# Weight operands kept as two pairs of tiles, raw-block products first, and the gated embedding added onto the output in DRAM

## The chip, the cores and the metric

The kernel runs on one NeuronCore of a Trainium2 chip: TensorE (PE) for matmuls, VectorE (DVE), ScalarE (ACT), GpSimd (POOL), and SyncE (SP), which here only issues DMAs. The metric is the device time of one execution in microseconds (us), as the median of the runs.

## The reference

One layer of a hybrid encoder for 640 tokens (512 of a prompt, 128 of samples): an input projection, attention beside a state-space group, and then the part that matters here, four large projections in fp32.

```python
merged = jnp.concatenate([rms_norm(attn, g_attn_out), rms_norm(ssm, g_ssm_out)], axis=-1)
h = x + merged @ w_out
f = rms_norm(h, g_ffn)
h = h + (jax.nn.silu(f @ w_gate) * (f @ w_up)) @ w_down
gate = jax.nn.sigmoid(rms_norm(h, g_ple) @ w_ple_gate)
h = h + gate * (p_i @ w_ple_proj)
```

D_MODEL is 2048 and D_FF 5632, so the weights of these four stages are 16 to 46 MB each and are read once.

## The kernel before

Up to about 806 us the kernel does the input projections, the attention and the state-space group. From there on it is one long sequence of 2x2 block multiplications by the Strassen-Winograd scheme: seven products in place of eight. The stages are called after the tiles that their products write: **o** (w_out, 8 cells of 4 units), **g** and **u** (w_gate and w_up, 22 pairs of cells of 4 units each), **d** (w_down, 28 cells of 2 to 4 units, the last eight with a longer ending), **p** (w_ple_gate, 8 cells of 4 units). That makes 87 cells that end in the function `strassen`, and a last one, p7, with code of its own.

A *unit* is a 128x1024 block of weights: four 128x256 quarters, loaded by SP into `wst` (two buffers, L60). For each unit:

- POOL makes three of the four weight sums in `ws` (L109, L110, L111), DVE the fourth (L112). `ws` has one buffer.
- ACT rounds each part to fp32r (`wh`, L86), and DVE takes the remainder (`wl`, L87). This is done once for the three raw quarters (128x768, straight from `wst`) and once for the four sums (128x1024, from `ws`). Below, these are the raw split and the sum split. Both write into one pair of tiles `wh`, `wl` of seven blocks, with two buffers: the pair of unit i+2 can be written only when PE is through with unit i.
- PE does seven products of six matmuls each, 42 matmuls of 128x320 per unit (L1205 to L1207). Products 1, 2 and 4 need raw quarters, products 3, 6, 7 and 5 need sums. The order is 1, 2, 3, 6, 7, 5, 4.

So the weights pass round a ring: POOL's three sums, ACT's sum split, DVE's sum split, and only then POOL's sums of the next unit, since `ws` has one buffer. Each product accumulates in its own PSUM bank over the units of a cell; there are eight banks. When a cell ends, the banks are read and combined (L1232 to L1240): 1 and 3 by ACT, the others by DVE, with one addition on POOL at the end (L1240). Then comes the stage's own ending: a row scale on DVE (`by_rows`, L1257), for g a Silu on ACT (L1307), for u a multiplication by g's tile on DVE (L1317) and four row sums on POOL (L118 to L121); for d an addition to `h_dr` in DRAM by a DMA that POOL issues (L1346), or in the last eight cells an addition, a scaling, squares and the row sums; for p a sigmoid (L1367), a multiplication by the projected embedding on DVE (L1370), the addition of the residual on POOL (L1373), and the store of the output.

The instructions are written cell by cell, but the order on each engine is set by a scheduler that runs at build time. Within an engine the instructions run strictly in that order.

## Time and profile before

| | |
|---|---|
| median of 3 runs | 3037.12 us (3029.13 to 3037.15) |
| the profiled execution, its own time | 3029.73 us |
| its span, first to last instruction | 3027.9 us |
| PE busy | 2850.7 us (94%) |
| DVE / POOL / ACT busy | 2042.4 / 1540.3 / 1237.7 us |
| mean granted TensorE clock | 0.983 of full |

The page's share of busy time says that PE is nearly always at work, but matmuls overlap in it, and its ends are modelled. Where PE stands still is better read from the start times of its matmuls: in an undisturbed run they start at an even distance, and what a stretch takes beyond its number of matmuls times that distance is lost. The page's chain of work that ended last passes through POOL for 23%, DVE for 15% and PE for 12% of the span.

### The profile page before, as it was taken

How to read it: one execution, taken by the hardware profiler on the slowest of the kernel's cores; microseconds unless marked ns; L12 is line 12 of the kernel's file. 1: busy time of each engine (PE TensorE's matmuls, PEld its weight loads, DVE VectorE, ACT ScalarE, POOL GpSimd, SP SyncE). 2: the span in 40 equal slices, each digit the busy share in tenths (PEclk: the TensorE clock that was granted, in tenths of full speed). 3: DMA queues.
4: the chain of work that ended last, by engine and by line, in shares of the span. 5: the costliest groups of instructions: out<-in, count | busy, mean ns of one | idle time of the engine just before them, and what ended most of it. 6: DMA issues, size and time to landing. Idle time of an engine off the chain costs nothing.

```text
span 3027.9 us, 48370 instructions
## 1 busy us (share of the span) xinstructions
PE 2850.7 (94%) x19051; PEld 2719.3 (90%) x19051; DVE 2042.4 (67%) x2830; ACT 1237.7 (41%) x1627; POOL 1540.3 (51%) x1545
## 2 busy tenths in 40 slices
PE   7899999999789889999999999999989999988898
PEld 6789988888788889999999999999989999987887
DVE  8939254455777786666666666666775667788766
ACT  4333365456633443333333333333434344444432
POOL 5612300000666665656565656565564554666665
PEclk9999999999899999999999999999999999999999
DMA  5565744456444623232323232323555455646443
GB/s 165 155 172 168 227 173 154 173 200 209 169 150 159 244 85 117 98 118 98 117 99 115 99 115 99 114 99 114 213 127 164 110 171 164 168 155 243 135 146 129
DMA packets 137494, 449.24 MB, mean 148 GB/s; under 512 B 14097, under 2 KB 34673, under 8 KB 124465
## 3 DMA queue, kind: packets, MB, share of 16 engines
q1 hardware_dynamic: 120032, 396.47, 38.6%
q0 software_dynamic: 15936, 45.47, 6.0%
q10 hardware_dynamic: 1296, 4.20, 0.4%
q8 instruction: 149, 2.44, 0.3%
q14 instruction: 81, 0.66, 0.1%
HBM read 342.25 MB, written 101.18 MB: 146 GB/s over the span
## 4 chain that ended last, share of the span: by engine, by line
POOL 23%; DVE 15%; PE 12%; issue 8%; ACT 6%; DMA 1%; DVEq 0%; POOLq 0%; SPq 0%; ACTq 0%
POOL ws L110 7%; DVE wl L87 7%; POOL ws L109 6%; ACT wh L86 5%; POOL ws L111 5%; PE d L1207 4%; PE d L1205 4%; PE d L1206 4%; POOL t L121 1%; POOL t L118 1%; DVE t L1257 1%; DVE rg L1257 1%; POOL rp L1373 1%; DVE kt L1051 1%; POOL t L120 1%
## 5 line engine op out<-in xcount | busy, mean ns | idle before, releaser
L86 ACT ACTIVATE wh<-ws 128x1024 fp32r<-128x1024 f32 x328 | 347.2, 1058 | 976.4 <-POOL ws L111 957.9
L87 DVE TENSOR_TENSOR wl<-ws,wh 128x1024 fp32r<-128x1024 f32 x328 | 415.9, 1268 | 488.2 <-ACT wh L86 488.0
L109 POOL TENSOR_TENSOR ws<-wst 128x256 f32<-128x256 f32 x328 | 335.4, 1023 | 758.1 <-DVE wl L87 758.1
L87 DVE TENSOR_TENSOR wl<-wst,wh 128x768 fp32r<-128x768 f32 x328 | 413.7, 1262 | 94.3 <-ACT wh L86 94.2
L1205 PE MATMUL d<-kt,wh 128*128 128x320 f32 x1232 | 384.9, 315 | 27.2 <-ACT wh L86 15.2
L1207 PE MATMUL g<-kf,wl 128*128 128x320 f32 x1232 | 380.6, 313 | 15.8 <-DVE wl L87 15.6
L1205 PE MATMUL g<-kf,wh 128*128 128x320 f32 x1232 | 382.1, 311 | 3.5 <-ACT wh L86 3.5
L1205 PE MATMUL u<-kf,wh 128*128 128x320 f32 x1232 | 380.7, 309 | 3.4 <-ACT wh L86 3.3
L1206 PE MATMUL d<-kt,wh 128*128 128x320 f32 x1232 | 381.9, 312 | 0.0
L1206 PE MATMUL g<-kf,wh 128*128 128x320 f32 x1232 | 381.4, 310 | 0.0
L1206 PE MATMUL u<-kf,wh 128*128 128x320 f32 x1232 | 380.3, 309 | 0.0
L1207 PE MATMUL u<-kf,wl 128*128 128x320 f32 x1232 | 379.4, 311 | 0.3 <-DVE wl L87 0.3
L1207 PE MATMUL d<-kt,wl 128*128 128x320 f32 x1232 | 362.6, 314 | 13.1 <-DVE wl L87 13.0
L110 POOL TENSOR_TENSOR ws<-ws,wst 128x256 f32<-128x256 f32 x328 | 357.3, 1089 | 23.1
L86 ACT ACTIVATE wh<-wst 128x768 fp32r<-128x768 f32 x328 | 275.0, 839 | 224.0 <-PE d L1206 74.2
L111 POOL TENSOR_TENSOR ws<-wst,ws 128x256 f32<-128x256 f32 x328 | 289.8, 884 | 21.2
L1205 PEld LDWEIGHTS d<-kt,wh 128*128 128x128 f32 x1232 | 234.8, 191 | 34.1 <-ACT wh L86 20.2
L1207 PEld LDWEIGHTS g<-kf,wl 128*128 128x128 f32 x1232 | 231.5, 189 | 22.9 <-DVE wl L87 22.2
L1207 PEld LDWEIGHTS d<-kt,wl 128*128 128x128 f32 x1232 | 228.6, 191 | 19.0 <-DVE wl L87 18.4
L1205 PEld LDWEIGHTS g<-kf,wh 128*128 128x128 f32 x1232 | 232.5, 189 | 5.3 <-ACT wh L86 5.2
L1205 PEld LDWEIGHTS u<-kf,wh 128*128 128x128 f32 x1232 | 231.3, 188 | 4.2 <-ACT wh L86 4.2
L1206 PEld LDWEIGHTS d<-kt,wh 128*128 128x128 f32 x1232 | 234.9, 191 | 0.0
(501 smaller groups left out, 6489.9 us busy)
## 6 DMA issues: line engine op xcount, KB each, us to landing
wst<-in_w_gate SPq DMA_DIRECT2D x88, 512.0 KB
wst<-in_w_up SPq DMA_DIRECT2D x88, 512.0 KB
wst<-in_w_down SPq DMA_DIRECT2D x88, 512.0 KB
tc_dr<-t SPq DMA_DIRECT2D x22, 1120.0 KB
kt<-tc_dr SPq DMA_DIRECT2D x22, 1120.0 KB
wst<-in_w_qk SPq DMA_DIRECT2D x32, 512.0 KB
kc<-in_cache_k SPq DMA_DIRECT2D x16, 1024.0 KB
vc<-in_cache_v SPq DMA_DIRECT2D x16, 1024.0 KB
```

The lines of the kernel that those rows point to most:

```text
L86: a = nc.scalar.activation(wh[:, part], x, AF.Copy)
L87: b = nc.vector.tensor_tensor(wl[:, part], x, wh[:, part].bitcast(F32), op=OP.subtract)
L109: tt(s[:, 0], q[:, 0], q[:, 3], op=OP.add)
L110: tt(s[:, 1], s[:, 0], q[:, 1], op=OP.subtract)
L111: tt(s[:, 3], q[:, 2], s[:, 1], op=OP.subtract)
L118: tt(s[:, 0], q[:, 0], q[:, 1], op=OP.subtract)
L120: tt(s[:, 1], q[:, 2], s[:, 0], op=OP.subtract)
L121: tt(s[:, 2], s[:, 1], q[:, 3], op=OP.subtract)
L1205: nc.tensor.matmul(ps[i], wh[:, a, w], k[:, 0, b], start=f, stop=False)
L1206: nc.tensor.matmul(ps[i], wh[:, a, w], k[:, 1, b], start=False, stop=False)
L1207: nc.tensor.matmul(ps[i], wl[:, a, w], k[:, 0, b], start=False, stop=l)
L1257: nc.vector.tensor_tensor(x, x, s[:, None, :].to_broadcast([P, 2, NTOK]), op=OP.mult)
```

## The change

There are three parts.

1. The seven blocks of `wh`, `wl` become two pairs of tiles, one of the three raw blocks (`whr`, `wlr`) and one of the four sums (`whs`, `wls`), each with two buffers. A new function `cut_blocks` does ACT's and DVE's step for one pair, and `split_raw` does the raw pair of unit i+2 while unit i is about to be multiplied.
2. The products run in the order 1, 2, 4, 3, 6, 7, 5, so that the three raw products come first. The banks are read in the same order: bank 4 is now read by ACT, negated, and a new POOL addition (r21 + r22) takes the place of DVE's subtraction.
3. In stage p the residual is no longer loaded and added on POOL. Stage d's last cells store the residual straight to the output `o_yT`, and p adds `z` onto it by an accumulating DMA that POOL issues. Only the last block pair keeps a DRAM tile of its own (`h7_dr`).

```diff
@@ Ring.split
-            wh = self.pool.tile([P, 7, 256], F32R, tag="w_h", name=f"wh{i}", bufs=2)
-            wl = self.pool.tile([P, 7, 256], F32R, tag="w_l", name=f"wl{i}", bufs=2)
             s = self.pool.tile([P, 4, 256], F32, tag="w_s", name=f"ws{i}", bufs=1)
...
             winograd_weights(nc, q, s)
-            for part, x in ((slice(0, 3), q[:, 1:]), (slice(3, 7), s)):
-                a = nc.scalar.activation(wh[:, part], x, AF.Copy)
-                b = nc.vector.tensor_tensor(wl[:, part], x, wh[:, part].bitcast(F32), op=OP.subtract)
-            self.done = (a.ins, b.ins)
+            raw = self.raw.pop(i, None) or self.cut_blocks(i, "r", q[:, 1:])
+            self.cut[i] = (raw, self.cut_blocks(i, "s", s))
+            self.load(i + 1 + STAGE)
+            return
...
+    def cut_blocks(self, i, kind, x):
+        n = x.shape[1]
+        h, l = (self.pool.tile([P, n, 256], F32R, tag=f"w_{part}{kind}", name=f"w{part}{kind}{i}", bufs=2)
+                for part in "hl")
+        a = self.nc.scalar.activation(h, x, AF.Copy)
+        b = self.nc.vector.tensor_tensor(l, x, h.bitcast(F32), op=OP.subtract)
+        self.done = (a.ins, b.ins)
+        return h, l
+
+    def split_raw(self, i):
+
+        if i < len(self.units) and self.units[i][0] == 1 and i not in self.cut and i not in self.raw:
+            self.load(i + 1)
+            self.raw[i] = self.cut_blocks(i, "r", self.st[i][0].rearrange("p (q n) -> p q n", q=4)[:, 1:])
@@ Ring.next
             self.split(i + 1)
+            if self.units[i][0] == 1:
+                self.split_raw(i + 2)
@@
-PRODUCTS = {1: (0, 1), 2: (1, 3), 3: (6, 2), 6: (4, 5), 7: (5, 0), 5: (3, 4), 4: (2, 6)}
+PRODUCTS = {1: (0, 1), 2: (1, 3), 4: (2, 6), 3: (6, 2), 6: (4, 5), 7: (5, 0), 5: (3, 4)}
@@ strassen
         tt(r11, q, ps[2], op=OP.add)
+        nc.scalar.activation(r21, ps[4], AF.Copy, scale=-1.0)
         nc.scalar.activation(r12, ps[3], AF.Copy)
         tt(q, q, ps[6], op=OP.add)
         tt(r22, q, ps[7], op=OP.add)
+        nc.gpsimd.tensor_tensor(r21, r21, r22, op=OP.add)
         tt(r12, r12, ps[5], op=OP.add)
-        tt(r21, r22, ps[4], op=OP.subtract)
@@ stage d, last cells
-        nc.sync.dma_start(rows(h2_dr, j), r)
+        nc.sync.dma_start(rows(io["o_yT"] if j < 7 else h7_dr, j % 7), r)
@@ stage p
         nc.vector.tensor_tensor(z, z, x, op=OP.mult)
-        x = pair(f"hy{j}")
-        nc.sync.dma_start(x, rows(h2_dr, j))
-        nc.gpsimd.tensor_tensor(z, z, x, op=OP.add)
-        nc.sync.dma_start(rows(io["o_yT"], j), z)
+        nc.gpsimd.dma_start(rows(io["o_yT"], j), z, accum_op=OP.add)
```

The scheduler orders the changed program anew. At three places this matters below. The number behind a tile's name is its unit or cell, then a serial number; lines of the changed kernel stand a few lines further on than in the one before.

DVE at the end of cell g10, before: the banks are read (L1233 to L1239), then come the raw split of unit 201, the row scale, and only then the sum split of unit 201.

```order
L1233 TENSOR_TENSOR rg10_15365<-qg10_15366,g10_2_15139 128x320
L112 TENSOR_TENSOR ws201_15354<-wst201_15253 128x256
L1235 TENSOR_TENSOR qg10_15366<-qg10_15366,g10_6_15141 128x320
L1236 TENSOR_TENSOR rg10_15365<-qg10_15366,g10_7_15142 128x320
L1237 TENSOR_TENSOR rg10_15365<-rg10_15365,g10_5_15143 128x320
L1238 TENSOR_TENSOR rg10_15365<-rg10_15365,g10_4_15144 128x320
L1239 TENSOR_TENSOR rg10_15365<-rg10_15365,g10_5_15143 128x320
L87 TENSOR_TENSOR wl201_15353<-wst201_15253,wh201_15352 128x768
L1257 TENSOR_TENSOR rg10_15365<-rg10_15365,ssqa_106 128x1280
L87 TENSOR_TENSOR wl201_15353<-ws201_15354,wh201_15352 128x1024
L112 TENSOR_TENSOR ws202_15430<-wst202_15308 128x256
```

The same place on DVE in the changed kernel (the row scale is L1274):

```order
L1249 TENSOR_TENSOR rg10_15629<-qg10_15630,g10_2_15395 128x320
L127 TENSOR_TENSOR ws201_15618<-wst201_15513 128x256
L95 TENSOR_TENSOR wlr201_15573<-wst201_15513,whr201_15572 128x768
L1252 TENSOR_TENSOR qg10_15630<-qg10_15630,g10_6_15398 128x320
L1253 TENSOR_TENSOR rg10_15629<-qg10_15630,g10_7_15399 128x320
L1255 TENSOR_TENSOR rg10_15629<-rg10_15629,g10_5_15400 128x320
L1256 TENSOR_TENSOR rg10_15629<-rg10_15629,g10_5_15400 128x320
L95 TENSOR_TENSOR wls201_15624<-ws201_15618,whs201_15623 128x1024
L1274 TENSOR_TENSOR rg10_15629<-rg10_15629,ssqa_106 128x1280
L127 TENSOR_TENSOR ws202_15697<-wst202_15570 128x256
```

One bank reading fewer stands there, the raw split has moved up, and the sum split now stands ahead of the row scale.

POOL in stage p after cell p3, before: the addition of the residual (L1373) stands between the first and the second sum of unit 399.

```order
L109 TENSOR_TENSOR ws397_27584<-wst397_27483 128x256
L110 TENSOR_TENSOR ws397_27584<-ws397_27584,wst397_27483 128x256
L1240 TENSOR_TENSOR rp3_27595<-rp3_27595,qp3_27596 128x320
L111 TENSOR_TENSOR ws397_27584<-wst397_27483,ws397_27584 128x256
L109 TENSOR_TENSOR ws398_27666<-wst398_27538 128x256
L110 TENSOR_TENSOR ws398_27666<-ws398_27666,wst398_27538 128x256
L111 TENSOR_TENSOR ws398_27666<-wst398_27538,ws398_27666 128x256
L109 TENSOR_TENSOR ws399_27721<-wst399_27593 128x256
L1373 TENSOR_TENSOR rp3_27595<-rp3_27595,hy3_27611 128x1280
L110 TENSOR_TENSOR ws399_27721<-ws399_27721,wst399_27593 128x256
```

The same place on POOL in the changed kernel (L1254 is the new addition, L1388 the accumulating DMA):

```order
L124 TENSOR_TENSOR ws397_28286<-wst397_28181 128x256
L125 TENSOR_TENSOR ws397_28286<-ws397_28286,wst397_28181 128x256
L126 TENSOR_TENSOR ws397_28286<-wst397_28181,ws397_28286 128x256
L1254 TENSOR_TENSOR rp3_28297<-rp3_28297 128x320
L1257 TENSOR_TENSOR rp3_28297<-rp3_28297,qp3_28298 128x320
L124 TENSOR_TENSOR ws398_28368<-wst398_28238 128x256
L125 TENSOR_TENSOR ws398_28368<-ws398_28368,wst398_28238 128x256
L126 TENSOR_TENSOR ws398_28368<-wst398_28238,ws398_28368 128x256
L1388 DMA o_yT<-rp3_28297 128x2x640
L124 TENSOR_TENSOR ws399_28425<-wst399_28295 128x256
```

Both combining additions stand after the third sum of unit 397, and the residual's addition has given way to a DMA issue after the third sum of unit 398.

ACT in the last cells of stage d, after cell d23, before: the sum split of unit 369 stands ahead of the cell's scaling and squares (L1267, L1249).

```order
L86 ACTIVATE wh368_25695<-ws368_25697 128x1024
L86 ACTIVATE wh369_25750<-wst369_25651 128x768
L86 ACTIVATE wh369_25750<-ws369_25752 128x1024
L1267 ACTIVATE hc7_25777<-rd23_25763,c_g_ple_136 128x640 x2
L1249 ACTIVATE hx7_25774<-rd23_25763 128x1280
L86 ACTIVATE wh370_25838<-wst370_25706 128x768
```

The same place on ACT in the changed kernel:

```order
L94 ACTIVATE whs368_26347<-ws368_26342 128x1024
L94 ACTIVATE whr370_26444<-wst370_26351 128x768
L1284 ACTIVATE hc7_26425<-rd23_26410,c_g_ple_136 128x640 x2
L1266 ACTIVATE hx7_26422<-rd23_26410 128x1280
L94 ACTIVATE whs369_26404<-ws369_26399 128x1024
```

The raw split of unit 370 and the cell's scaling and squares now stand ahead of the sum split of unit 369.

## Rows read from the trace of the kernel before

**Rows 1.** Stretches by stage: us; busy us (instructions) by engine; PEclk, DMA share, GB/s.
```profile
806.00:1052.00 246.00, 213.17 (x1344) 205.22 (x1343) 184.49 (x182) 104.06 (x128) 164.91 (x149) 0.94 0.49 172
1052.00:1110.00 58.00, 45.93 (x270) 42.96 (x270) 51.48 (x50) 32.40 (x36) 34.44 (x26) 0.91 0.35 132
1110.00:2140.00 1030.00, 1018.24 (x6880) 1008.67 (x6879) 700.20 (x800) 354.42 (x430) 613.12 (x614) 1.00 0.32 107
2179.00:2600.00 421.00, 399.58 (x2644) 395.09 (x2644) 284.43 (x347) 165.97 (x200) 228.88 (x234) 0.98 0.53 151
2600.00:2786.00 186.00, 166.31 (x1066) 157.61 (x1066) 149.53 (x156) 85.08 (x103) 124.42 (x113) 0.99 0.56 190
2786.00:3018.00 232.00, 210.36 (x1337) 198.90 (x1336) 162.55 (x174) 86.34 (x101) 141.34 (x113) 0.99 0.45 149
```

**Rows 2.** Timeline of PE: start, us, instruction; the first and 88th of 88 even matmuls.
```profile
1307.22 0.31 PE L1207 MATMUL u<-kf,wl 128*128 128x320 f32 x1
...
1319.98 0.31 PE L1207 MATMUL u<-kf,wl 128*128 128x320 f32 x1
```

**Rows 3.** Timeline of PE, stages g and u: the one stall of each pair, twice.
```profile
1237.73 0.42 PE L1207 MATMUL g<-kf,wl 128*128 128x320 f32 x1 [0.60 <-DVE wl L87]
...
1288.05 0.41 PE L1207 MATMUL g<-kf,wl 128*128 128x320 f32 x1 [0.60 <-DVE wl L87]
```

**Rows 4.** Timeline of POOL, ACT and DVE: one undisturbed turn of the ring.
```profile
1312.36 0.98 POOL L109 TENSOR_TENSOR ws<-wst 128x256 f32<-128x256 f32 x1 [2.43 <-DVE wl L87]
...
1314.84 0.73 POOL L111 TENSOR_TENSOR ws<-wst,ws 128x256 f32<-128x256 f32 x1
1315.60 1.06 ACT L86 ACTIVATE wh<-ws 128x1024 fp32r<-128x1024 f32 x1 [3.77 <-POOL ws L111]
1316.69 1.23 DVE L87 TENSOR_TENSOR wl<-ws,wh 128x1024 fp32r<-128x1024 f32 x1 [2.54 <-ACT wh L86]
1318.00 0.97 POOL L109 TENSOR_TENSOR ws<-wst 128x256 f32<-128x256 f32 x1 [2.43 <-DVE wl L87]
```

**Rows 5.** Timeline of POOL and DVE: the turn in which a cell of g ends.
```profile
1299.89 0.74 POOL L109 TENSOR_TENSOR ws<-wst 128x256 f32<-128x256 f32 x1 [2.43 <-DVE wl L87]
...
1304.01 1.48 DVE L1257 TENSOR_TENSOR rg<-rg,ssqa 128x1280 f32<-128x1280 f32 x1
1305.41 1.22 DVE L87 TENSOR_TENSOR wl<-ws,wh 128x1024 fp32r<-128x1024 f32 x1
1306.70 0.98 POOL L109 TENSOR_TENSOR ws<-wst 128x256 f32<-128x256 f32 x1 [3.44 <-DVE wl L87]
```

**Rows 6.** Timeline of POOL: the two turns in which a cell of u ends.
```profile
1323.64 0.75 POOL L109 TENSOR_TENSOR ws<-wst 128x256 f32<-128x256 f32 x1 [2.43 <-DVE wl L87]
...
1330.46 1.92 POOL L109 TENSOR_TENSOR ws<-wst 128x256 f32<-128x256 f32 x1 [3.44 <-DVE wl L87]
...
1337.27 1.73 POOL L121 TENSOR_TENSOR t<-t 128x320 f32<-128x320 f32 x1
1338.97 0.92 POOL L109 TENSOR_TENSOR ws<-wst 128x256 f32<-128x256 f32 x1
```

**Rows 7.** Timeline of PE, DVE and POOL in stage p: one period between equal stalls.
```profile
2903.13 0.41 PE L1205 MATMUL p<-kh,wh 128*128 128x320 f32 x1 [0.73 <-ACT wh L86]
...
2917.36 2.03 DVE L1370 TENSOR_TENSOR rp<-rp,pj 128x1280 f32<-128x1280 f32 x1
...
2924.77 3.68 POOL L1373 TENSOR_TENSOR rp<-rp,hy 128x1280 f32<-128x1280 f32 x1
...
2931.12 0.42 PE L1205 MATMUL p<-kh,wh 128*128 128x320 f32 x1 [0.45 <-ACT wh L86]
```

**Rows 8.** Groups of POOL's instructions, 806 to 3028 us: busy us, mean ns | idle before.
```profile
L1346 POOL DMA_DIRECT2D h_dr<-rd x20 | 24.1, 1205 | 13.5 <-DVE rd L1239 10.2 <-POOL rd L1240 2.2 <-POOL ws L111 1.0
L1240 POOL TENSOR_TENSOR t<-t,qu 128x320 f32<-128x320 f32 x22 | 20.8, 947 | 1.0
```

**Rows 9.** Chain of work that ended last, in order of time: a weight load.
```profile
2019.89 4.83 DMA wst<-in_w_gate
```

More of the change, by code (lines that the diff above doesn't have):

```diff
@@ L50, in __init__ @@
         self.pool = None
-        self.loaded, self.st, self.cut, self.pos = 0, {}, {}, 0
+        self.loaded, self.st, self.cut, self.raw, self.pos = 0, {}, {}, {}, 0
     def load(self, upto):
@@ L79, in split @@
         else:
-            wh = self.pool.tile([P, 7, 256], F32R, tag="w_h", name=f"wh{i}", bufs=2)
-            wl = self.pool.tile([P, 7, 256], F32R, tag="w_l", name=f"wl{i}", bufs=2)
+            q = t.rearrange("p (q n) -> p q n", q=4)
             s = self.pool.tile([P, 4, 256], F32, tag="w_s", name=f"ws{i}", bufs=1)
-            q = t.rearrange("p (q n) -> p q n", q=4)
             winograd_weights(nc, q, s)
-            for part, x in ((slice(0, 3), q[:, 1:]), (slice(3, 7), s)):
-                a = nc.scalar.activation(wh[:, part], x, AF.Copy)
-                b = nc.vector.tensor_tensor(wl[:, part], x, wh[:, part].bitcast(F32), op=OP.subtract)
-            self.done = (a.ins, b.ins)
+            raw = self.raw.pop(i, None) or self.cut_blocks(i, "r", q[:, 1:])
+            self.cut[i] = (raw, self.cut_blocks(i, "s", s))
+            self.load(i + 1 + STAGE)
+            return
         self.cut[i] = (wh, wl)
         self.load(i + 1 + STAGE)
+    def cut_blocks(self, i, kind, x):
[10 more added lines that the diff above has]
+            self.raw[i] = self.cut_blocks(i, "r", self.st[i][0].rearrange("p (q n) -> p q n", q=4)[:, 1:])
     def ahead(self):
@@ L197, in hybrid_step @@
     h_dr = dp.tile([D, NTOK], F32, name="h_dr")
-    h2_dr = dp.tile([D, NTOK], F32, name="h2_dr")
+    h7_dr = dp.tile([2 * P, NTOK], F32, name="h7_dr")
     tc_dr = dp.tile([FT // 2, P, 7, NH2], F32, name="tc_dr")
@@ L1199, in product @@
             a, b = PRODUCTS[i]
-            wh, wl = cut
+            wh, wl = cut[a > 2]
+            a -= 3 * (a > 2)
             for c in range(2):
@@ L1379, in hybrid_step @@
     nc.sync.dma_start(x, rows(pj_dr, 7))
-    nc.sync.dma_start(y, rows(h2_dr, 7))
+    nc.sync.dma_start(y, rows(h7_dr, 0))
     ps = products("p7", hk, order=(1, 2, 6, 5, 3, 7, 4))
```

## The prediction

> **What bounds the kernel now.** I read four views: the busy time by stage, the starts of PE's matmuls, what its stalls wait for, and the turns of the ring on POOL, ACT and DVE.
>
> First PE's floor. The stretches by stage give the number of matmuls in each [rows 1]. In an even run 88 of them start from 1307.22 to 1319.98 us [rows 2]: 12.76 / 87 = 0.1467 us each, so a unit of 42 costs 6.16 us, a cell of four units 24.64, a pair g, u 49.28. Set against the stretches, PE loses 246 - 1344 x 0.1467 = 49 us in stage o, 18 in the first pair (1052 to 1110), 21 in the even part of g and u, 33 in the first part of d, 30 in d's last cells, 36 in p: 187 us in all. No instruction of PE is saved, so this is all that can be won, and the part of it that goes to loading and splitting operands at the start of o, g and d is not touched by the change. In g and u there is one stall per pair, a wait for DVE's sum split, and it repeats after 1288.05 - 1237.73 = 50.32 us, 1.0 over the floor [rows 3].
>
> Then the ring. An undisturbed turn takes 1318.00 - 1312.36 = 5.64 us [rows 4]: POOL's three sums, ACT's sum split 1.06, DVE's sum split 1.23, and POOL stands idle 2.43 of it, waiting for DVE. PE's unit takes 6.16, so four turns (22.56) have only 2.1 us to spare in a cell for anything else that gets between. In g and u they do not have it: the turn in which g ends takes 6.81 [rows 5], those in which u ends 6.82 and 8.51 [rows 6], with five plain ones 50.3 us: the period of PE's stalls. The ring, not PE, sets the pace there. In p the period is 2931.12 - 2903.13 = 27.99 [rows 7] against 24.64.
>
> It follows that tolerance alone buys little: what counts in a steady stage is how many turns' worth of work the ring does per cell, and whether that is under PE's floor.
>
> **The change part by part.** *Products and bank readings.* Sums are needed after three products instead of two, 0.88 us later in a unit. PE's idle 0.60 at each g [rows 3] would be covered by that if the ring kept up on average. DVE loses one bank reading per cell, ACT gains one; ACT is idle 3.77 before its sum split [rows 4], which hides it.
>
> *POOL's new addition.* 87 cells times 0.95, the mean of the addition beside it [rows 8], are 83 us of POOL time, on an engine of the ring. I cost it at nothing, because both additions now stand behind the third sum, where POOL idles 2.43 anyway [rows 4], and 2 x 0.95 = 1.9 fits. The cover is gone if bank 7 is read more than 0.5 us after that sum: then POOL's next sums, queued behind the addition, are late by as much (rival A).
>
> *g and u.* In the turn where g ends, DVE's sum split waited behind the row scale (1.48) [rows 5]. It now stands ahead of it, so the turn falls from 6.81 to about 5.64; likewise u's first, from 6.82. But the row scale then runs beside POOL's next first sum. The nearest row is the sum of 1.92 instead of 0.98 at u's end [rows 4, 6]: +0.95. At u's second turn the multiplication stands before the sum split and POOL's last row sum (1.73) [rows 6] moves between the next unit's sums: about +0.4 over the two turns. Net -1.17 - 1.18 + 0.95 + 0.4 = -1.0, a ring of 49.3: level with PE's floor. I take -0.8 for each of 21 pairs, **-17** (bounds 0 and -21).
>
> By the Trainium skill, "SBUF — State Buffer", section "Who interferes with whom", a DVE instruction with two SBUF inputs and a GpSimd instruction that reads SBUF shut each other out for a whole instruction. The row agrees in kind, but the sum grew by 0.95, less than the 1.48 of the row scale. With the full 1.48 per pair the term would be some -6.
>
> *p.* The residual's addition goes: 3.68 on POOL, between two sums of a unit [rows 7]. In its place POOL issues a DMA, 1.2 us after a wait of 0.7 (24.1 and 13.5 over 20) [rows 8]. New period: four turns, 22.56; the additions hidden; the row scale and the 2.03 multiplication [rows 7] ahead of the sum split, with bounds 0 and +1.0; the DMA issue behind that multiplication, which makes POOL's next sum late by 1.0 to 1.8. That gives 23.6 to 25.4, so PE's 24.64 takes over; allowing 0.3 for leftover stalls the period falls by 3.0, over six full periods **-18** (bounds -8 and -21). SP loses two DMAs per cell, and the weight loads move up by these. The accumulation has a whole period, 24 us, until its buffer is needed; I cost it at nothing.
>
> *o.* The ending has what d's last cells have: an addition, a scaling, squares, row sums. The additions on POOL are hidden; the sum split no longer stands behind a bank reading. Against that, scaling and squares now precede the next sum split. I take -1.3 for seven cells, **-9** (bounds +7, and -25 if the ring drops to PE's floor).
>
> *d, first part.* Cells of four units were at the floor but for operand splits; POOL gets the addition and the DMA of 1.2 behind the third sum, 2 x 0.95 + 0.7 + 1.2 = 3.8 against 2.43 idle, which eats 1.4 of the 2.1 to spare. Some stalls behind operand splits shrink with the 0.88. **-4** (bounds +10 and -15).
>
> *d, last eight cells.* Here the raw split of unit 370 and the whole scaling and squares stand before the sum split of 369. The raw split needs a weight buffer that is only free once unit 368 is summed, and a load takes 4.83 at an idle time [rows 9], longer beside the traffic here (190 GB/s) [rows 1]. So ACT can stand still for about 5 us with the ring behind it, where it used to go on. PE's own order helps: raw products of a later unit precede the sums of an earlier one. **-4** (bounds +8, and -25 at the floor). The first pair: **-1** (0 to -5).
>
> **The sum.** -17 - 18 - 9 - 4 - 4 - 1 = -53. Against the profiled execution's own 3029.7 us that is 2977. Two of the three runs shown lie 7.4 above it, so the median may; I predict **2980 us**. My own range for this case is 2945 to 3012.
>
> **The rivals.** *A, the addition lands on the ring (slower).* At each cell's end POOL waits in order for the reading of bank 7, with the next unit's sums queued behind. For it: the ring has no spare time in g and u [rows 3], so whatever is late on POOL is late on PE. Against it: bank 7 is now the last but one, and DVE reads it before its sum split, which POOL must wait for anyway. If all 87 land, 2977 + 83 = 3060 us; slower than before from about three quarters of them.
>
> *B, PE everywhere.* The raw pair is ready early, so even o and d fall to PE's floor: g and u -21, p -25, o -25, d -40, the first pair -5, together -116 or 2914 us. For it: the raw split drops out of the way of PE, which needs it first, and 0.88 us is more than most single stalls. Against it: in o and d nothing shortens the long turn in which a cell ends.
>
> *C, given back.* Only p and a little of g and u are won (-10, -6), while early raw splits make ACT wait for weight loads in o and in d's last cells, about +1 per cell (+15): 3029 us, no change. For it: [rows 9] and the order on ACT. Against it: in g, u and p the order keeps each raw split directly ahead of its own sum split, as before.
>
> **How the numbers follow.** Forecast 0.60, A 0.10, B 0.14, C 0.16. The range of 8 in 10 leaves out A and half of B: 2915 to 3032. A measurement of this kernel can tell about 0.3%, 9 us, from no change. Faster: the forecast, B and a third of C, 0.80; the same: half of C, 0.08; slower: A and the rest, 0.12.
>
> **What would show it.** In the changed trace: the stalls of g and u every 49.3 to 49.6 us instead of 50.32; in p a period near 24.9 and POOL's DMA issue near 1.2; the new addition followed at once by the second, with POOL still waiting for DVE at the next first sum. If POOL's wait names instead DVE's reading of bank 7 or ACT's of bank 4 ahead of the addition, A is right. If the last cells of d take over 22 us with ACT waiting for a load, C is. What would make me wrong most easily is the long turn in o and d, which I could bound only widely.

## The result, and the profile of the changed kernel

The changed kernel is slower, by less than 1%: a median of 3057.6 us (3057.5 to 3059.69) against 3036.16 for the kernel before in the same comparison, a ratio of 1.0078 with a 95% interval of 1.0065 to 1.009. The prediction was 2980 us with a range up to 3032, and "faster" at 0.80. The profiled execution has 3057.61 us, its span is 3055.8, 27.9 more than before.

From the page of the changed kernel: the span, the busy times, the chain that ended last, and two groups of the ring (columns: instruction and count | busy us, mean ns of one | idle time ahead of it and what ended that).

```profile
span 3055.8 us, 48777 instructions
...
PE 2854.3 (93%) x19051; PEld 2711.7 (89%) x19051; DVE 2082.2 (68%) x2743; ACT 1258.5 (41%) x1714; POOL 1665.5 (55%) x1632
...
L95 DVE TENSOR_TENSOR wls<-ws,whs 128x1024 fp32r<-128x1024 f32 x328 | 427.7, 1304 | 455.1 <-ACT whs L94 454.7
L124 POOL TENSOR_TENSOR ws<-wst 128x256 f32<-128x256 f32 x328 | 364.7, 1112 | 609.2 <-DVE wls L95 609.2
```

POOL is busy for 1665.5 us instead of 1540.3: the new addition (87 times, 90.6 us together) and longer instructions. The stretches by stage, as in [rows 1] (us; busy us and instructions by engine; granted clock, DMA share, GB/s):

```profile
809.00:1052.00 243.00, 210.90 (x1352) 202.54 (x1351) 186.92 (x177) 107.98 (x137) 175.29 (x156) 0.96 0.48 175
1110.00:2172.00 1062.00, 1029.34 (x6878) 1008.53 (x6877) 736.86 (x759) 359.87 (x471) 690.19 (x655) 1.00 0.30 104
2211.00:2640.00 429.00, 404.38 (x2657) 394.72 (x2656) 291.93 (x327) 173.11 (x222) 263.14 (x254) 0.98 0.51 151
2640.00:2828.00 188.00, 163.90 (x1062) 155.61 (x1062) 142.84 (x149) 86.63 (x110) 137.46 (x121) 1.00 0.55 184
2828.00:3049.00 221.00, 204.88 (x1333) 200.02 (x1331) 166.36 (x176) 91.17 (x111) 127.32 (x122) 0.96 0.47 139
```

The even part of g and u has the same number of matmuls as before (6878 and 6880) but takes 1062 us instead of 1030, at the full granted clock both times. Stage p, the last row, takes 221 instead of 232. So the loss sits in g and u, and there is a gain in p. The stall that recurs once per pair, to be set beside [rows 3]:

```profile
1245.02 0.41 PE L1223 MATMUL g<-kf,wls 128*128 128x320 f32 x1 [0.71 <-DVE wls L95]
...
1296.98 0.41 PE L1223 MATMUL g<-kf,wls 128*128 128x320 f32 x1 [0.70 <-DVE wls L95]
```

It repeats after 51.96 us instead of 50.32, where 49.3 to 49.6 was predicted. It is no longer the only stall: by the starts of its matmuls PE now loses 2.7 us per pair instead of 1.0, at some four places. PE still waits for DVE's sum split, so the ring still sets the pace, and it has become slower. These are the turns of the steady pair, from one first sum on POOL to the next (read from the timeline), beside what the prediction's steps say for them:

| turn | before | predicted | after |
|---|---|---|---|
| in which g ends | 6.81 | 5.64 | 6.43 |
| the next | 5.66 | 6.6 | 6.66 |
| two plain ones | 11.28 | 11.28 | 11.29 |
| in which u ends | 6.82 | 5.64 | 6.44 |
| the next two | 14.09 | 14.5 | 15.50 |
| one plain | 5.64 | 5.64 | 5.65 |
| pair | 50.30 | 49.3 | 51.97 |

Three turns miss: the two in which a cell ends, by 0.8 each, and those behind u's end, by 1.0. Here is the end of a cell of g on POOL and DVE (start, duration, instruction, and in brackets the wait ahead of it and what ended it):

```profile
1302.65 0.72 POOL L124 TENSOR_TENSOR ws<-wst 128x256 f32<-128x256 f32 x1 [2.43 <-DVE wls L95]
...
1305.57 0.49 DVE L1253 TENSOR_TENSOR rg<-qg,g 128x320 f32<-128x320 f32 x1
...
1306.20 0.88 POOL L1254 TENSOR_TENSOR rg<-rg 128x320 f32<-128x320 f32 x1 [0.54 <-DVE rg L1253]
...
1307.04 0.88 POOL L1257 TENSOR_TENSOR rg<-rg,qg 128x320 f32<-128x320 f32 x1
1307.11 0.49 DVE L1256 TENSOR_TENSOR rg<-rg,g 128x320 f32<-128x320 f32 x1 [0.66 <-POOL rg L1254]
1307.52 1.48 DVE L95 TENSOR_TENSOR wls<-ws,whs 128x1024 fp32r<-128x1024 f32 x1
1308.93 1.48 DVE L1274 TENSOR_TENSOR rg<-rg,ssqa 128x1280 f32<-128x1280 f32 x1
1309.08 1.92 POOL L124 TENSOR_TENSOR ws<-wst 128x256 f32<-128x256 f32 x1 [1.16 <-DVE wls L95]
```

L1253 writes q + bank 7 into r22. POOL's new addition L1254 reads r22. DVE's next update of r22, L1256, adds bank 5 **onto the same r22**, so it may not start before POOL has read it: 0.66 us of DVE standing still. The sum split L95 is queued behind L1256 on DVE, and POOL's next first sum waits for the sum split. So a short addition on an engine that was idle holds up the ring by way of an overwrite, on the other engine. And u's end, from the last of a round of sums to the first of the next:

```profile
1336.35 1.33 POOL L126 TENSOR_TENSOR ws<-wst,ws 128x256 f32<-128x256 f32 x1
1337.01 2.03 DVE L1334 TENSOR_TENSOR t<-t,rg 128x1280 f32<-128x1280 f32 x1
...
1339.11 1.80 POOL L133 TENSOR_TENSOR t<-t 128x320 f32<-128x320 f32 x1 [1.43 <-DVE t L1334]
...
1341.90 1.59 POOL L135 TENSOR_TENSOR t<-t 128x320 f32<-128x320 f32 x1
1343.45 0.73 POOL L124 TENSOR_TENSOR ws<-wst 128x256 f32<-128x256 f32 x1
```

The multiplication L1334 now stands ahead of a sum split and ends late. POOL idles 1.43 us for it after its sums, and then three row sums (L133 to L135, 4.3 us) stand between two rounds of weight sums. Before, the multiplication stood behind a sum split and the row sums lay around POOL's sums; the turn took 8.51.

At the start of p there is a third loss. PE stands at the two matmuls that sum the squares of the stage (one for each half of the tokens), which the order places between p's products. The first waits for the squares, the second for DVE's scaling of the first sum (L1052):

```profile
2846.30 1.43 PE L1050 MATMUL pm<-ssq,onesr 128*128 128x320 f32 x2 [3.53 <-DVE ssq L1271]
2851.24 1.44 PE L1050 MATMUL pm<-ssq,onesr 128*128 128x320 f32 x2 [3.50 <-DVE ssq L1052]
```

Before, the same matmuls did not wait. Two things differ: counted from the reading of bank 1 in d's last cell, the squares end at 31.2 us instead of 26.8, and the order places both matmuls behind 84 of p0's 168, where before they stood behind 102 and 116. Which of the two makes PE wait is not separated.

### The profile page after: what moved, and what is told of

It reads as the page before. It is cut to its first block, busy times and chain, and to the rows that moved or that the text cites. A ratio compares the mean times of both kernels' runs of the same rounds, so it can differ in the third digit from the quotient of the medians.

```text
span 3055.8 us, 48777 instructions
## 1 busy us (share of the span) xinstructions
PE 2854.3 (93%) x19051; PEld 2711.7 (89%) x19051; DVE 2082.2 (68%) x2743; ACT 1258.5 (41%) x1714; POOL 1665.5 (55%) x1632
## 3 DMA queue, kind: packets, MB, share of 16 engines
q1 hardware_dynamic: 116224, 387.29, 36.4%
## 4 chain that ended last, share of the span: by engine, by line
POOL 21%; DVE 15%; PE 13%; issue 9%; ACT 5%; DMA 2%; POOLq 0%; DVEq 0%; SPq 0%; ACTq 0%
POOL ws L124 5%; POOL ws L125 5%; DVE wls L95 5%; ACT whs L94 4%; POOL ws L126 4%; DVE wlr L95 4%; PE d L1223 2%; PE d L1221 2%; PE d L1222 2%; PE p L1223 2%; PE p L1221 2%; PE p L1222 2%; DVE kt L1066 1%; DVE t L1334 1%; POOL t L133 1%
## 5 line engine op out<-in xcount | busy, mean ns | idle before, releaser
L94 ACT ACTIVATE whs<-ws 128x1024 fp32r<-128x1024 f32 x328 | 347.3, 1059 | 1013.0 <-POOL ws L126 997.2
L95 DVE TENSOR_TENSOR wls<-ws,whs 128x1024 fp32r<-128x1024 f32 x328 | 427.7, 1304 | 455.1 <-ACT whs L94 454.7
L95 DVE TENSOR_TENSOR wlr<-wst,whr 128x768 fp32r<-128x768 f32 x328 | 460.7, 1405 | 71.8 <-ACT whr L94 63.2
L94 ACT ACTIVATE whr<-wst 128x768 fp32r<-128x768 f32 x328 | 273.3, 833 | 170.5 <-DMA wst<-in_w_down 85.0
L127 DVE TENSOR_TENSOR ws<-wst 128x256 f32<-128x256 f32 x328 | 231.0, 704 | 6.9 <-DMA wst<-in_w_out 1.8
L1223 PE MATMUL g<-kf,wls 128*128 128x320 f32 x704 | 218.7, 313 | 16.2 <-DVE wls L95 16.2
L1221 PE MATMUL d<-kt,whs 128*128 128x320 f32 x704 | 220.0, 315 | 14.7 <-ACT whs L94 7.4
L1221 PE MATMUL g<-kf,whs 128*128 128x320 f32 x704 | 220.7, 314 | 10.4 <-ACT whs L94 10.4
L1221 PE MATMUL u<-kf,whs 128*128 128x320 f32 x704 | 217.8, 309 | 1.4 <-ACT rg L1251 1.0
L1223 PE MATMUL u<-kf,wls 128*128 128x320 f32 x704 | 216.6, 310 | 1.5 <-DVE wls L95 1.5
L1222 PE MATMUL g<-kf,whs 128*128 128x320 f32 x704 | 218.0, 310 | 0.0
L1222 PE MATMUL u<-kf,whs 128*128 128x320 f32 x704 | 217.4, 309 | 0.0
L1222 PE MATMUL d<-kt,whs 128*128 128x320 f32 x704 | 216.5, 310 | 0.0
L1221 PE MATMUL d<-kt,whr 128*128 128x320 f32 x528 | 164.7, 314 | 15.9 <-ACT whr L94 13.8
```

Of the source, the lines that this page charges most:

```text
L94: a = self.nc.scalar.activation(h, x, AF.Copy)
L95: b = self.nc.vector.tensor_tensor(l, x, h.bitcast(F32), op=OP.subtract)
L127: nc.vector.tensor_tensor(s[:, 2], q[:, 1], q[:, 0], op=OP.subtract)
L1221: nc.tensor.matmul(ps[i], wh[:, a, w], k[:, 0, b], start=f, stop=False)
L1222: nc.tensor.matmul(ps[i], wh[:, a, w], k[:, 1, b], start=False, stop=False)
L1223: nc.tensor.matmul(ps[i], wl[:, a, w], k[:, 0, b], start=False, stop=l)
```

## The experiments

All times of stages below are counted from ACT's reading of bank 1 in one cell, its mark, to the same reading in another: "d, first 20" is from d0 to d20, "d, last 8" from d20 to d27, "to p0" from d27 to p0, "p" from p0 to p7. One execution of each kernel was traced; where two kernels have the same order of instructions in a stage, they differ there by up to some 3 us. The ratio is that to the kernel before, run beside it. "Pair" is the period of g and u.

| kernel | ratio (95%) | pair | o | g, u | d, first 20 | d, last 8 | to p0 | p |
|---|---|---|---|---|---|---|---|---|
| before | 1 | 50.30 | 195.0 | 1088.3 | 426.5 | 155.6 | 36.5 | 196.2 |
| after | 1.0078 (1.0065 to 1.009) | 51.97 | 188.5 | 1121.4 | 438.0 | 152.0 | 49.3 | 174.7 |
| e1_combine_alone | 1.021 (1.0194 to 1.0225) | 51.77 | 198.9 | 1120.8 | 429.5 | 167.1 | 40.1 | 205.2 |
| e2_pairs_alone | 1.0056 (1.0039 to 1.0072) | 51.87 | 192.0 | 1120.6 | 438.4 | 150.2 | 40.7 | 180.3 |
| e3_dram_alone | 0.9936 (0.9921 to 0.9951) | 50.30 | 195.1 | 1088.3 | 425.2 | 155.7 | 36.5 | 181.9 |
| e4_own_tile | 1.003 (1.0017 to 1.0043) | 51.06 | 186.8 | 1105.2 | 429.8 | 156.6 | 47.0 | 179.3 |
| e8_dve_subtract | 1.0012 (1.0003 to 1.0022) | 51.98 | 188.2 | 1120.3 | 432.4 | 156.6 | 33.9 | 173.8 |
| e7_no_early_raw | 1.0073 (1.0057 to 1.0089) | 51.94 | 189.1 | 1117.5 | 437.5 | 154.4 | 48.1 | 175.2 |
| e13_mult_only | 1.0048 (1.0033 to 1.0063) | 51.57 | 188.7 | 1115.0 | 438.3 | 150.5 | 49.9 | 175.8 |
| e5_mult_late | 0.9935 (0.9919 to 0.9951) | 49.85 | 188.2 | 1079.8 | 431.3 | 153.8 | 48.7 | 179.4 |
| e9_sums_dve | 0.9852 (0.9835 to 0.9868) | 49.28 | 194.6 | 1063.6 | 425.9 | 155.8 | 36.4 | 181.9 |
| e10_pairs_sums_dve | 0.9803 (0.9788 to 0.9817) | 49.04 | 187.9 | 1061.9 | 427.1 | 157.1 | 37.2 | 172.1 |
| e11_o_sums_dve | 0.9784 (0.9767 to 0.98) | 49.28 | 182.7 | 1064.3 | 426.3 | 155.8 | 36.3 | 182.2 |
| e12_all | 0.9759 (0.9744 to 0.9773) | 49.04 | 183.6 | 1061.0 | 427.7 | 156.7 | 36.2 | 172.4 |

The marks are not at the same place of PE's work in every kernel: from d20's mark to d27's, PE starts 898 matmuls in the kernel before and 861 in the changed one. So the single stages are better compared by what they take beyond their matmuls, at 0.14667 us each (the distance that e9_sums_dve keeps over 14 pairs without a gap; a lower granted clock counts as loss too):

| us beyond the matmuls | o | g, u | d, first 20 | d, last 8 | to p0 | p0 to the end |
|---|---|---|---|---|---|---|
| before | 26.3 | 27.0 | 28.8 | 23.9 | 16.0 | 34.6 |
| after | 21.6 | 60.6 | 38.3 | 25.7 | 21.1 | 15.5 |
| e2_pairs_alone | 22.2 | 57.6 | 32.2 | 22.9 | 16.8 | 22.9 |
| e3_dram_alone | 26.9 | 27.0 | 27.4 | 24.0 | 15.9 | 15.7 |
| e4_own_tile | 19.9 | 44.4 | 29.2 | 31.5 | 20.2 | 18.6 |
| e8_dve_subtract | 21.0 | 60.3 | 27.6 | 27.3 | 11.6 | 16.2 |
| e12_all | 11.3 | 3.8 | 22.9 | 27.3 | 13.9 | 13.8 |

**The three parts, each alone.** The theory to test was the overwrite; its rivals, that POOL's added time or the early raw splits cost the time.

e1_combine_alone: the kernel before with the order of products and the cell's end of the changed kernel.

```diff
-PRODUCTS = {1: (0, 1), 2: (1, 3), 3: (6, 2), 6: (4, 5), 7: (5, 0), 5: (3, 4), 4: (2, 6)}
+PRODUCTS = {1: (0, 1), 2: (1, 3), 4: (2, 6), 3: (6, 2), 6: (4, 5), 7: (5, 0), 5: (3, 4)}
...
+        nc.scalar.activation(r21, ps[4], AF.Copy, scale=-1.0)
...
+        nc.gpsimd.tensor_tensor(r21, r21, r22, op=OP.add)
...
-        tt(r21, r22, ps[4], op=OP.subtract)
```

> The kernel before with the new order of products, bank 4 read negated by ACT and the addition on POOL; one weight tile and DRAM as before. Overwrite theory (DVE's second update of r22 must wait until POOL has read it, and the sum split is queued behind it): two delayed cell ends per pair, so the period of g and u rises from 50.32 to 51.5 to 52.5 and the kernel is 25 to 45 us slower than before, about 3070. If the loss came from the split weight pair instead, the period stays at 50.3 or less and the kernel is within 10 us of before.

The period is as the overwrite theory says, 51.77; both turns in which a cell ends take 7.55 instead of 6.81, which is all of it. The timeline of POOL and DVE at a cell's end:

```profile
1318.64 0.89 POOL L1238 TENSOR_TENSOR rg<-rg 128x320 f32<-128x320 f32 x1
...
1319.56 0.49 DVE L1240 TENSOR_TENSOR rg<-rg,g 128x320 f32<-128x320 f32 x1 [0.91 <-POOL rg L1238]
...
1322.50 1.21 DVE L87 TENSOR_TENSOR wl<-ws,wh 128x1024 fp32r<-128x1024 f32 x1
```

DVE has one subtraction of 0.49 less, but waits 0.91 for POOL, and the raw split beside POOL's second addition takes 1.21 instead of 0.95. The total is worse than expected (63 us, not 25 to 45): d's last cells and p lose too, 11.5 and 9 by the marks.

e2_pairs_alone: the kernel before with only the pairs of tiles and `split_raw`, the first part of the change.

```diff
-            wh = self.pool.tile([P, 7, 256], F32R, tag="w_h", name=f"wh{i}", bufs=2)
-            wl = self.pool.tile([P, 7, 256], F32R, tag="w_l", name=f"wl{i}", bufs=2)
...
+            raw = self.raw.pop(i, None) or self.cut_blocks(i, "r", q[:, 1:])
+            self.cut[i] = (raw, self.cut_blocks(i, "s", s))
...
+                self.split_raw(i + 2)
```

> The kernel before with the two pairs of weight tiles and the early raw split; order of products, cell's end and DRAM as before. Overwrite theory: g and u keep their 50.3 period (nothing in the cell's end is changed). Theory of the early raw splits (rival C): stage o and d's last cells lose, by waits of ACT for weight loads, +5 to +20 us together, so 3040 to 3055 in all. If the pairs were to blame for the loss in g and u, the period there is near 52 and the time near 3065.

The period is 51.87, as the last branch of the expectation has it, though nothing at the cell's end is changed; the overwrite theory alone would have left it at 50.3. (The time is 3047.67 us, not 3065, because o and p gain.) The scheduler's order has moved on ACT. ACT and DVE where a cell of g ends:

```profile
1300.81 2.02 DVE L1273 TENSOR_TENSOR rg<-rg,ssqa 128x1280 f32<-128x1280 f32 x1
1302.86 1.27 ACT L1323 ACTIVATE rg<-rg 128x1280 f32<-128x1280 f32 x1 [5.01 <-DVE rg L1273]
1304.04 1.04 ACT L94 ACTIVATE whs<-ws 128x1024 fp32r<-128x1024 f32 x1
```

The Silu now stands ahead of ACT's sum split and waits for DVE's row scale; POOL's sums had been there since 1301.48. That turn takes 7.97. So a split of the weight pair alone costs as much in g and u as the whole change, by another way. The parts are therefore not additive: each of the first two alone adds 1.5 to a pair, both together 1.7. From p0 to the end the pairs alone bring 11.7 us.

e3_dram_alone: the kernel before with only the third part of the change.

```diff
-        nc.sync.dma_start(rows(h2_dr, j), r)
+        nc.sync.dma_start(rows(io["o_yT"] if j < 7 else h7_dr, j % 7), r)
...
-        nc.gpsimd.tensor_tensor(z, z, x, op=OP.add)
-        nc.sync.dma_start(rows(io["o_yT"], j), z)
+        nc.gpsimd.dma_start(rows(io["o_yT"], j), z, accum_op=OP.add)
```

> The kernel before with the residual left on the output in DRAM and added there by an accumulating DMA; nothing else changed. All theories: everything up to p as before, p's period falls from 27.99 to 24.7 to 25.5, so p takes 215 to 222 us instead of 232 and the kernel 3018 to 3026. If p's gain came from the new cell's end instead, p stays near 28 per cell and the time within 5 us of before.

As expected, and a little better: p's period is 24.9 in its last four cells, everything ahead of p is unchanged within 2 us, and the kernel takes 3011.81 us. The third part alone is a gain.

**What of the changed kernel costs the time in g and u.** In the steady pairs of g and u each of the next kernels differs from its base only in the instructions of its edit and their place; the rest of ACT's, DVE's and POOL's order is the same. In d and p the scheduler orders anew. e4_own_tile gives q + bank 7 a tile of its own:

```diff
-        tt(r22, q, ps[7], op=OP.add)
-        nc.gpsimd.tensor_tensor(r21, r21, r22, op=OP.add)
+        w = fo.tile([P, NH2], F32, tag="w", name="w" + name, bufs=1)
+        tt(w, q, ps[7], op=OP.add)
+        nc.gpsimd.tensor_tensor(r21, r21, w, op=OP.add)
         tt(r12, r12, ps[5], op=OP.add)
-        tt(r22, r22, ps[5], op=OP.add)
+        tt(r22, w, ps[5], op=OP.add)
```

> The changed kernel, with q + bank 7 written to a tile of its own, which POOL's addition and DVE's second update both read, so that no overwrite is waited for. Overwrite theory: the period of g and u falls from 51.97 to about 50.4 (two times 0.8 less), o and d gain a little, 3010 to 3028 in all. If POOL's own time, or DVE and POOL shutting each other out, is to blame: 51.5 to 52 and 3047 to 3060.

The kernel is about 15 us faster by the ratios (1.0078 to 1.003), and the period falls by 0.91, about half of what the overwrite theory says. The end of a cell of g:

```profile
1303.25 0.48 DVE L1257 TENSOR_TENSOR rg<-wg,g 128x320 f32<-128x320 f32 x1
...
1303.67 1.37 DVE L95 TENSOR_TENSOR wls<-ws,whs 128x1024 fp32r<-128x1024 f32 x1
1303.91 1.86 POOL L1258 TENSOR_TENSOR rg<-rg,qg 128x320 f32<-128x320 f32 x1
1305.74 0.73 POOL L124 TENSOR_TENSOR ws<-wst 128x256 f32<-128x256 f32 x1
```

The wait is gone, and DVE's sum split starts as soon as ACT's has ended. But POOL's second addition now falls beside it and takes 1.86 instead of 0.88, and the next first sum starts behind that addition, 0.7 after the sum split's end: the addition itself lies on the ring. The turn is 6.21 instead of 6.43, and the next one 6.00 instead of 6.66, since other pairs of instructions meet. Behind u's end nothing is gained (10.18 instead of 9.98).

e8_dve_subtract undoes the addition altogether:

```diff
-        nc.scalar.activation(r21, ps[4], AF.Copy, scale=-1.0)
...
-        nc.gpsimd.tensor_tensor(r21, r21, r22, op=OP.add)
         tt(r12, r12, ps[5], op=OP.add)
+        tt(r21, r22, ps[4], op=OP.subtract)
```

> The changed kernel with DVE's subtraction of bank 4 as in the kernel before, so that neither ACT's negated reading nor POOL's new addition exists; pairs, order of products and DRAM stay. Overwrite theory: no engine reads r22 beside DVE, the sum split follows the last bank reading at once, and DVE has 0.49 us more per cell; the period of g and u falls from 51.97 to 50.9 to 51.4, 3030 to 3046 in all. If the loss lies in the order of products or the pairs, not in the addition: within 6 us of the changed kernel.

The kernel is as fast as that of before, but the period stays at 51.98, against the expectation. DVE's subtraction takes the place of DVE's wait, to within 0.04 us per turn (6.47 and 6.65 instead of 6.43 and 6.66):

```profile
1299.87 0.73 POOL L124 TENSOR_TENSOR ws<-wst 128x256 f32<-128x256 f32 x1 [2.43 <-DVE wls L95]
1300.80 1.49 DVE L95 TENSOR_TENSOR wlr<-wst,whr 128x768 fp32r<-128x768 f32 x1
...
1304.14 0.48 DVE L1255 TENSOR_TENSOR rg<-rg,g 128x320 f32<-128x320 f32 x1
1304.31 0.87 POOL L1256 TENSOR_TENSOR rg<-rg,qg 128x320 f32<-128x320 f32 x1 [1.44 <-DVE rg L1254]
1304.54 1.72 DVE L95 TENSOR_TENSOR wls<-ws,whs 128x1024 fp32r<-128x1024 f32 x1
```

So moving this step from DVE to POOL gained nothing in g and u: what DVE was relieved of, it spent waiting. The rows also show why the turn does not come down to the 5.64 of a plain one, with or without the addition. Here DVE works with hardly a gap (0.1 at most) until the sum split starts, 4.67 after POOL's first sum (4.33 in the plain turn of [rows 4]): the raw split now stands ahead of most bank readings, beside POOL's second sum, and takes 1.49. In the kernel before it stood behind them and took less:

```profile
1303.14 0.95 DVE L87 TENSOR_TENSOR wl<-wst,wh 128x768 fp32r<-128x768 f32 x1
```

Then the sum split itself takes 1.72 instead of 1.23, beside POOL's addition. The row scale is out of the turn, and about 1.0 of its 1.4 us is taken by these two.

The 20 us that this kernel gains over the changed one lie in d's first 20 cells (10.7 less beyond the matmuls) and between d27 and p0 (9.5 less). At p0 the sum of the squares stands behind 143 of the 168 matmuls here, and PE does not wait for it, nor in e2_pairs_alone; in e1_combine_alone and e4_own_tile, which have the addition, it does (2.98 us, and 1.27 with 4.13).

e7_no_early_raw takes out the call that makes the early raw split:

```diff
-            if self.units[i][0] == 1:
-                self.split_raw(i + 2)
```

> The changed kernel without the early raw split (split_raw): the pairs of tiles, the order of products, the cell's end and DRAM stay. Rival C (early raw splits make ACT wait for weight loads in o and d): ACT's waits for loads go back to about 5 us in all, d's first part falls from 438 to about 430 us and o by a few, 3040 to 3050 in all, with the period of g and u still near 52 because of the overwrite wait. If the early splits cost nothing: within 6 us of the changed kernel, or slower, since the raw split then stands with the sum split again behind the row scale (period 51.8 to 52.5).

The time does not change, but the run does not test what it was meant to test. The scheduler moves the raw splits ahead by itself: in o, and from d0 to the end, ACT, DVE, POOL and PE run the same instructions in the same order as in the changed kernel, and only the first pairs of g and u differ. In d's last eight cells the raw split of the next unit still stands ahead of all 20 sum splits. What ACT's raw split waited for, in the changed kernel (us in total, times, longest):

```profile
ACT whr L94 <- DMA wst<-in_w_down: 85.0, 38, 5.1
ACT whr L94 <- DMA wst<-in_w_out: 40.1, 20, 2.6
```

and in this one:

```profile
ACT whr L94 <- DMA wst<-in_w_down: 93.7, 41, 5.2
ACT whr L94 <- DMA wst<-in_w_out: 39.4, 21, 2.7
```

The waits for loads that rival C foretold are there (in the kernel before, 5.1 us on w_out and 0.7 on w_pg; on w_pg in the changed kernel 25.6, the longest 11.1). They go with the early order on ACT: in e8, where the next raw split stands ahead of 11 of d's sum splits instead of 50, they are 21.1 on w_down (and 29.0 on w_out). But they take the place of other waits. These are the raw split's rows from the pages of the kernel before and the changed one, with the idle time ahead of it last:

```profile
L86 ACT ACTIVATE wh<-wst 128x768 fp32r<-128x768 f32 x328 | 275.0, 839 | 224.0 <-PE d L1206 74.2
L94 ACT ACTIVATE whr<-wst 128x768 fp32r<-128x768 f32 x328 | 273.3, 833 | 170.5 <-DMA wst<-in_w_down 85.0
```

Before, ACT waited mostly for PE to be through with an older unit; now it comes earlier to a load that has not landed, and idles less in all. Whether the early order costs time in d is open: the kernels that have less of it (e8, e12) lose less in d's first 20 cells, but they lack POOL's addition too.

**The place of u's multiplication.** e5_mult_late is e4_own_tile with u's ending written into the next cell, behind its second unit's sum split:

```diff
+        if kind == "s":
+            self.sums = b.ins
...
-        nc.vector.tensor_tensor(t, t, z, op=OP.mult)
-        keep(nc.gpsimd, c, tc_dr, f)
+        def held(u, c=c, t=t, z=z, f=f):
+            if u == 1:
+                with tc.issue_after(ring.sums):
+                    nc.vector.tensor_tensor(t, t, z, op=OP.mult)
+                keep(nc.gpsimd, c, tc_dr, f)
...
```

> The changed kernel with the tile of its own for q + bank 7 (as in e4_own_tile), and u's multiplication and row sums moved behind the next sum split, which is where they stand in the kernel before. Theory of the second cause (the multiplication ahead of the sum split makes POOL's row sums start 1.4 us after its sums are through, so that they stand between two rounds of sums): e4's period of 51.06 falls by 0.6 to 0.9, to 50.2 to 50.5, and the kernel is 12 to 19 us faster than e4_own_tile, 3021 to 3029. If DVE's and POOL's shutting each other out costs the same wherever the multiplication stands: 50.9 to 51.2 and 3037 to 3043.

More than expected: the period falls by 1.21 to 49.85, under that of the kernel before. On POOL the row sums (here L135 to L138, since two lines were added above) lie around the sums again:

```profile
1331.78 1.92 POOL L126 TENSOR_TENSOR ws<-wst 128x256 f32<-128x256 f32 x1 [2.43 <-DVE wls L95]
...
1334.54 1.59 POOL L135 TENSOR_TENSOR t<-t 128x320 f32<-128x320 f32 x1
1336.10 0.73 POOL L128 TENSOR_TENSOR ws<-wst,ws 128x256 f32<-128x256 f32 x1
...
1340.29 0.92 POOL L126 TENSOR_TENSOR ws<-wst 128x256 f32<-128x256 f32 x1
```

The turns behind u's end are 6.00 and 8.53, together with the next plain one 20.1 instead of 21.3.

e13_mult_only makes the same move in the changed kernel, with r22 as one tile.

> The changed kernel with only u's multiplication and row sums moved back behind the next sum split; r22 stays one tile, so the overwrite wait remains. If the two causes add up (the place of the multiplication 1.2 per pair, as from e4_own_tile to e5_mult_late; the overwrite 0.9): the period of g and u falls from 51.97 to 50.6 to 50.9, 3028 to 3036 in all. If the multiplication's place matters only when the overwrite wait is gone: 51.5 to 52 and 3048 to 3058.

It brings 0.40 per pair, not 1.2: the two causes do not add up. The turns show why. With the overwrite the turn behind a cell's end is 6.64, without it 6.00, at g's end and at u's. Behind u's end POOL's wait for the multiplication covered that difference in the changed kernel, so e4_own_tile gained only at g (0.91) and the move alone only 0.40; once the multiplication is out of the way, the overwrite costs 1.72 per pair (51.57 to 49.85).

**Toward a faster kernel.** If POOL's row sums are what makes u's second turn long, they should go to DVE. e9_sums_dve is e3_dram_alone with

```diff
-        keep(nc.gpsimd, c, tc_dr, f)
+        keep(nc.vector, c, tc_dr, f)
```

> The kernel before with the DRAM part alone (as e3_dram_alone) and u's four row sums on DVE instead of POOL. If POOL's row sums are what makes u's second turn long (8.51 against 5.64): the period of g and u falls from 50.30 towards PE's floor of 49.28, to 49.3 to 49.8, 2990 to 3001 in all. If four more DVE instructions of 0.48 ahead of the sum split cost as much: 50.2 to 50.6 and 3008 to 3018.

The period is 49.28, PE's floor by the prediction's count, and the kernel is at 0.9852 of the one before. On the fullest engine of the ring the row sums cost less than on POOL:

```profile
1326.25 1.02 DVE L118 TENSOR_TENSOR t<-t 128x320 f32<-128x320 f32 x1
...
1328.61 0.48 DVE L119 TENSOR_TENSOR t<-t 128x320 f32<-128x320 f32 x1
...
1330.55 0.48 DVE L121 TENSOR_TENSOR t<-t 128x320 f32<-128x320 f32 x1
```

Together 2.5 us, against 5.1 on POOL in the kernel before. The same edit on e8_dve_subtract is e10_pairs_sums_dve:

> e8_dve_subtract (pairs, order of products and DRAM of the changed kernel, subtraction on DVE) with u's row sums on DVE. If POOL's row sums are what make u's second turn long whatever the combination: the period of g and u falls from 51.98 to 49.3 to 50.3 and the kernel to 2975 to 3002. If DVE is by then the engine that is full in that turn: 50.5 to 51.5 and 3005 to 3030.

2974.79 us; the period falls from 51.98 to 49.04. e11_o_sums_dve and e12_all also move o's row sums, in e9 and in e10:

```diff
-            keep(nc.gpsimd, c, fc_dr, j)
+            keep(nc.vector, c, fc_dr, j)
```

> e9_sums_dve with the row sums of stage o on DVE too. If POOL's row sums hold up the ring in o as they do in u: 1 to 3 us less per cell, seven cells, 2968 to 2983 in all. If DVE, which adds the residual and the squares there, is the full engine: 2986 to 3000.

> e10_pairs_sums_dve with the row sums of stage o on DVE too. By what o does in e11_o_sums_dve: the same gain, so 5 to 20 us under e10, or none if DVE is the full engine there.

2968.43 and 2961.63 us. Beyond its matmuls stage o loses 14 and 9 us less, and the way from its last cell to g's first 4 and 1 less. The last kernel keeps the pairs, the order of products and the accumulation in DRAM, and puts the subtraction and the row sums on DVE; it beats both kernels, by 2.4% and 3.2%. Its busy times:

```profile
PE 2828.9 (96%) x19051; PEld 2716.9 (92%) x19051; DVE 2169.0 (73%) x2946; ACT 1240.5 (42%) x1627; POOL 1448.5 (49%) x1429
```

and its even stretch of g and u, 1020 us with 6953 matmuls, 0.1467 us each as in [rows 2]:

```profile
1110.00:2130.00 1020.00, 1019.82 (x6953) 1019.45 (x6952) 811.64 (x893) 361.95 (x436) 569.49 (x540) 1.00 0.33 112
```

DVE is busier than in either kernel, and in this stretch PE loses nothing to the ring any more. (The page's chain that ended last says nothing here: its shares add up to some 6% of the span, so it reaches back only to 2749 us, near the start of p.)

## Why the prediction was wrong, point by point

- **What bounds the kernel: right.** The ring sets the pace in g and u [rows 3], and PE's floor is 49.28 per pair, which e9 and e11 reach. In e10 and e12 the marks on ACT are 49.04 apart: the ring itself now turns faster than PE and gains on it (4683 matmuls lie between marks 14 pairs apart in e10, not 14 x 336 = 4704), while PE's matmuls start 0.1467 apart without a gap. No kernel gets under the floor.
- **g and u, -17: it was +33, and here is the step that failed.** The turn "falls from 6.81 to about 5.64" was mis-sized, twice per pair: it takes 6.43, and 1.6 of the 2.7 us that a pair misses are here. The row scale does leave that turn, but the prediction took out its 1.48 and counted what is left as a plain turn. It is not plain: bank readings, the raw split (1.48 instead of 0.95) and the sum split (1.48 instead of 1.22) keep DVE, and in the changed kernel 0.66 of waiting for POOL comes on top. Without the wait the turn is 6.21 (e4), without the addition 6.47 (e8). The next turn was right (6.6; 6.66). Behind u's end, 14.5 was predicted and 15.50 measured: the prediction saw that the multiplication moves ahead of the sum split, but not that POOL then waits for it with three row sums still to do. With both mended (e5) the term is -8.5, half of what was predicted.
- **"POOL's new addition. I cost it at nothing": wrong.** It was costed on POOL's own queue, where it does fit: only 0.54 us of waiting stands ahead of it. Not looked at was who else uses its operand. DVE writes r22 again right behind, the sum split is queued behind that, and the wait comes back through DVE. Against a tile of its own the overwrite costs 0.91 per pair in this kernel (e4), 16 us over the stage, and DVE's relief by one subtraction is used up by it (e8: 51.98). Undoing the addition also gives back 10.7 us in d's first 20 cells and 9.5 between d27 and p0 (e8), but there the scheduler's order changes with it.
- **p, -18: right.** POOL's DMA issue took 1.19 us where 1.2 was assumed, the period from p0 to p6 falls by 2.9 on average (24.6 to 25.1 in the last three cells, 25.8 to 29.2 before them), and beyond its matmuls the stage loses 19.1 us less to the end. The third part alone gives 18.9 of it (e3). The pairs alone would have given 11.7 (e2), and the two do not add up.
- **Where d passes into p** the prediction had no term: 5.1 us beyond the matmuls. (The marks have 12.8, but PE starts 192 matmuls between them, not 140 as before.)
- **o, -9: right in direction, half in size.** The cells lose 4.7 us less beyond their matmuls (6.5 by the marks). Its reasons were not tested.
- **d: -4 for the first part was +9.5 beyond the matmuls** (+11.5 by the marks, where its bound was +10). e4, with a tile of its own, has 9.1 of it back, though with another order in d. The pairs alone add 3.4 (e2). **The last eight cells, -4:** -3.6 by the marks, but +1.8 beyond the matmuls, so the match is luck.
- **Rival A** had the direction and nearly the time (3060), and the row that it named is there: ahead of the addition POOL waits for DVE's reading of bank 7. But so is the row that was to speak for the forecast: the second addition follows at once, and POOL still waits for DVE at the next first sum. The two did not exclude each other. A's price, 83 us for additions queued on POOL, is not what happened: the whole addition undone gives 20 us back (e8), and part of the loss lies in the place of the multiplication.
- **Rival C** foretold ACT's waits for loads, and six of d's last seven periods did take 22.0 to 23.9 us with them. But in the kernel before six of the seven took 21.6 to 25.0 without them. Its cause was not tested, since e7 leaves the early order as it was; for d's first 20 cells it stays open.
- **Rival B**, PE's floor everywhere, holds in g and u once the row sums leave POOL; o and d stay above it (e12 still loses 11.3 us in o and 50 in d beyond the matmuls).

The sum, beyond the matmuls: 33.6 in g and u, 9.5 and 1.8 in d, 5.1 into p, -19.1 from p0 on, -4.7 in o, and some 1.6 in the pieces between and ahead, together 27.8 us; the span grew by 27.9.

## What to carry to other kernels

Before an operation goes to an idle engine, list who writes its operands next: an update in place on the old engine turns into a wait for the new one, and everything that is queued behind it pays. Here, in g and u, that wait cost as much as the subtraction had cost on the old engine. When an instruction is moved out of a turn, add up what is left there, lengthened by its new neighbours, before calling the turn a plain one. Where two engines and a single buffer form a ring, count each turn's work on both, with what gets between, rather than the idle time of the one that receives. The fuller engine can be the right place: a DVE instruction of 0.5 us took the place of a POOL instruction of 0.9 to 1.8 us, and PE's stalls went.
